# Half-size products on pairs of 512-column blocks and 8 of 16 chunks, one ring of weight buffers, and the running sum in DRAM

## The chip, the cores and the metric

The kernel runs on one core of one Trainium2 chip. The metric is the device time of one execution in microseconds (us); the median of three runs of the kernel before is 1694.32 us (1693.03 to 1695.05). A core has TensorE (PE, with its weight load PEld), VectorE (DVE), ScalarE (ACT), GpSimd (POOL) and SyncE (SP); each works through a queue of its own in order, and they wait for each other by semaphores. The big loads are issued by SP.

## The reference

One layer of a decoder trunk on 256 tokens of width D = 2048, in float32:

```python
proj = rmsnorm(x, attn_norm) @ w_in          # q, k, v of three mixers, and the gates (3 x 2048)
y_gla, y_sb, y_mem = (mixer(...) @ w_br for each of the three branches)
g = sigmoid(gates)
merged = g[0] * y_gla + g[1] * y_sb + g[2] * y_mem
x = x + merged @ w_o
gate, up = split(rmsnorm(x, ffn_norm) @ w_gate_up)      # 2 x 5632 columns
x = x + (silu(gate) * up) @ w_down
```

Nearly all the work is in products of 256 tokens with weight matrices that are read once from DRAM.

## The kernel before, in words

**Tiling.** Weights lie in blocks of 512 columns (NB); a chunk is 128 rows of a weight matrix. A block of `w_gate`, `w_o` or `w_gate_up` has 16 chunks, and `w_down` is taken in parts of 16, 16 and 12 chunks. Tokens are two halves of 128. The activation, stored transposed, is PE's stationary operand, the weights stream through.

**Precision.** Every float32 operand is split into a rounded part `h` (float32r) and a remainder `l`, and a product is three matmuls: h*h, h*l, l*h. For the weights this happens on the chip: `split` (L118) lets ScalarE cast a loaded tile to `wh` (L121) and VectorE subtract, `wl = raw - wh` (L122).

**Plain products.** `gemm` (L152) takes four chunks to a load (`raw`, 1 MB), two to a split of 1024 elements per partition, and issues 12 matmuls of 512 columns for each split.

**Products with fewer multiplications.** `sgemm` (L183) works on one block of 512 columns. Its first 6 chunks and the 256 tokens are cut in half every way (128 tokens, 3 chunks, 256 columns), and seven products of such halves stand for eight (the Winograd form of Strassen's method). The four quarters of the weights (`b11` to `b22`, tag `rq`, five buffers of 384 KB) are loaded apart, and VectorE adds them in place four times (L252, 768 elements per partition) between the splits. Each product (`prod`, L218) is 9 matmuls of 256 columns; the results are kept in `cv` by ScalarE and joined on VectorE at the block's end (L297, L302). The other 10 chunks of the block are done by `rest` (L230), as in a plain product. The sums on the token side, the forms, are made once for each activation by `make_forms` (L305) in two `raw` buffers.

**Order.** The program is written out in order; each engine's order comes from a scheduler of the framework that weighs the written order against its own times. `background` holds small jobs (transposes of finished pieces, the forms), and each product and each split of a gemm lets one step of them through (`step`, L98).

**Buffers.** `raw` has three slots. The pairs `wh`/`wl` have 4 buffers in the first stage (pool `wring`) and 6 in the later ones (pools `mrg` and `ffn`, released and made anew at L843, L896 and L900). PSUM holds 4 `acc` and 4 `tmp`.

**The stages the change touches.** The gates of two branches (L854 to L868): `sgemm` on a gate block, then a `gemm` with the branch's weights. The output product (L877 to L889), with the residual added into `x2`, which stays in SBUF. The FFN (L905 to L934): three parts, each with 4, 4 or 3 pairs of gate and up blocks, then that part of `w_down` added into `x2`; the last part (12 chunks) uses `gemm`.

Of the kernel before, what the change touches and what calls it, by code (L numbers as in the profile page):

```python
# [16 lines left out]
P = 128  # L17
# [13 lines left out]
SP = 3  # L31
HB = NB // 2
# [43 lines left out]
def trunk(ctx: ExitStack, tc: tile.TileContext, a, out):  # L76
# [5 lines left out]
    wp = ctx.enter_context(tc.tile_pool(name="wp", bufs=3))  # L82
    IT = 2 * NB
    small = ctx.enter_context(tc.tile_pool(name="small", bufs=2))
# [60 lines left out]
    def loads():  # L145
        return wp.tile([P, KG, NB], F32, tag="raw", name="raw", bufs=3)

    def parts():

        return [kit.tile([P, IT], F32R, tag=f"w{x}", name=f"w{x}", bufs=ring_bufs) for x in "hl"]  # L150

    def gemm(xs, w, c0, row0=0, first=(), load=nc.sync.dma_start):  # L152
# [9 lines left out]
        for n in sizes:  # L162
            xp = [x() if callable(x) else x for x in xs[k0 : k0 + n]]
            raw = loads()
            r0 = row0 + k0
            load(raw[:, :n], w[c0 // NB, :, r0 : r0 + n])
            for g in range(0, n, 2):
                m = min(2, n - g)
                wh, wl = (x[:].rearrange("p (k n) -> p k n", k=2) for x in parts())
                split(wh[:, :m], wl[:, :m], raw[:, g : g + m])  # L170
                for t in range(2):
                    s = slice(t * P, (t + 1) * P)
                    for j in range(m):
                        xh, xl = xp[g + j]
                        k = k0 + g + j
                        pe.matmul(o[t][:], xh[:, s], wh[:, j], start=k == 0, stop=False)  # L176
                        pe.matmul(o[t][:], xh[:, s], wl[:, j], start=False, stop=False)  # L177
                        pe.matmul(o[t][:], xl[:, s], wh[:, j], start=False, stop=k == nk - 1)  # L178
                step()
# [3 lines left out]
    def sgemm(xs, forms, w, blk, row0=0, late=False):  # L183
# [11 lines left out]
        o = [acc() for _ in range(2)]  # L195
        x = tmp()
        cv = kit.tile([P, 5, HB], F32, tag="cv", name="cv", bufs=2)
        wb = w[blk, :, row0 * NB : (row0 + nk) * NB]
        ob = 4 * SP * HB

        def quarter(i):
            q = kit.tile([P, SP * HB], F32, tag="rq", name="rq", bufs=5)
            nc.sync.dma_start(q[:], wb[:, i * SP * HB : (i + 1) * SP * HB])
            return q

        def form(src):
            hi, lo = (x[:, : SP * HB] for x in parts())
            split(hi, lo, src[:])
            return hi, lo

        def single(half, tok):
            s = slice(tok * P, (tok + 1) * P)
            return [[part[:, s] for part in xs[half * SP + i]] for i in range(SP)]

        def formed(f):
            return [[part[:, f, i] for part in forms] for i in range(SP)]

        def prod(dst, left, right, start=False, stop=False):  # L218
            hi, lo = right
            for i in range(SP):  # L220
                xh, xl = left[i]
                c = slice(i * HB, (i + 1) * HB)
                pe.matmul(dst, xh, hi[:, c], start=start and i == 0, stop=False, skip_group_check=True)  # L223
                pe.matmul(dst, xh, lo[:, c], start=False, stop=False, skip_group_check=True)  # L224
                pe.matmul(dst, xl, hi[:, c], start=False, stop=stop and i == SP - 1, skip_group_check=True)  # L225
            step()

        loaded = {}

        def rest(k0, last=False):  # L230

            if k0 not in loaded:
                n = min(KG, nk - k0)
                raw = loads()
                c = ob + (k0 - 2 * SP) * NB
                nc.sync.dma_start(raw[:, :n], wb[:, c : c + n * NB].rearrange("p (k n) -> p k n", n=NB))
                for g in range(0, n, 2):
                    loaded[k0 + g] = raw[:, g : g + 2]
            wh, wl = (x[:].rearrange("p (k n) -> p k n", k=2) for x in parts())
            split(wh, wl, loaded[k0])  # L240
            for t in range(2):
                s = slice(t * P, (t + 1) * P)
                for j in range(2):
                    xh, xl = xs[k0 + j]
                    f, e = k0 + j == 2 * SP, last and j == 1
                    pe.matmul(o[t][:], xh[:, s], wh[:, j], start=f, stop=False, skip_group_check=True)  # L246
                    pe.matmul(o[t][:], xh[:, s], wl[:, j], start=False, stop=False, skip_group_check=True)  # L247
                    pe.matmul(o[t][:], xl[:, s], wh[:, j], start=False, stop=e, skip_group_check=True)  # L248
            step()

        def add(dst, a, b):
            dve.tensor_tensor(dst[:], a[:], b[:], op=ALU.add)  # L252

        ks = list(range(2 * SP, nk, 2))
        x0, x1 = x[:, :HB], x[:, HB:]

        def some():
            if ks and not late:
                rest(ks[0], len(ks) == 1)
                ks.pop(0)  # L260

        if late:
            for j in ks:
                rest(j)
        some()
        b21 = quarter(0)
        prod(x0, single(1, 0), form(b21), start=True, stop=True)
        act.copy(cv[:, 2], x0)
        b11 = quarter(2)
        prod(o[0][:, :HB], single(0, 0), form(b11))  # L270
        b22 = quarter(1)
        some()
        add(b21, b21, b22)
        prod(x1, formed(1), form(b21), stop=True)
        b12 = quarter(3)
        prod(o[0][:, HB:], formed(0), form(b12), stop=late)
        some()
        add(b22, b22, b12)
        add(b12, b12, b21)
        prod(x0, formed(2), form(b12), stop=True)  # L280
        act.copy(cv[:, 4], x0)
        some()

        def p7():
            prod(x0, formed(3), form(b22), stop=True)
            act.copy(cv[:, 0], x0)

        def q4():
            add(b11, b11, b12)
            prod(o[1][:, :HB], single(0, 1), form(b11), stop=late)  # L290

        for f in (q4, p7) if late else (p7, q4):
            f()
        while ks and not late:
            some()

        dve.tensor_tensor(  # L297
            cv[:, 1:4:2], x1.unsqueeze(1).to_broadcast([P, 2, HB]), cv[:, 0:5:4], op=ALU.subtract
        )
        c = [cv[:, i : i + 2].rearrange("p a b -> p (a b)") for i in (2, 0)]  # L300
        for t in range(2):
            dve.tensor_tensor(c[t], o[t][:], c[t], op=ALU.add)  # L302
        return c

    def make_forms(parts, name):  # L305


        sf = [kit.tile([P, 4, SP, P], F32R, name=f"{name}{x}", bufs=1) for x in "hl"]

        def flat():  # L310
            return loads()[:].rearrange("p g n -> p (g n)")[:, : 2 * SP * T]

        def make():
            hw = flat().rearrange("p (k t) -> p k t", k=2 * SP)
            r = flat().rearrange("p (f i t) -> p f i t", f=4, i=SP)
            k = 0
            for h, l in parts:
                n = min(h.shape[1], 2 * SP - k)
                dve.tensor_tensor(hw[:, k : k + n], h[:, :n].bitcast(F32), l[:, :n].bitcast(F32), op=ALU.add)
                k += n  # L320
            yield
            a11, a12, a21, a22 = (hw[:, k * SP : (k + 1) * SP, i * P : (i + 1) * P] for i in range(2) for k in range(2))
            s3, s5, s6, s7 = (r[:, f] for f in range(4))
            dve.tensor_tensor(s5, a22, a21, op=ALU.subtract)
            dve.tensor_tensor(s7, a12, a22, op=ALU.subtract)
            dve.tensor_tensor(s6, s5, a12, op=ALU.subtract)
            dve.tensor_tensor(s3, a11, s6, op=ALU.add)
            yield
            split(sf[0][:], sf[1][:], r)
            yield  # L330

        background.append(make())
        return sf
# [27 lines left out]
    def token_rstd(name, src, r, n):  # L361

        ss = const.tile([P, 2], F32, name=f"{name}_ss")
        for t in range(2):
            x = loads()[:].rearrange("p g n -> p (g n)")
            nc.sync.dma_start(x, src[t * P : (t + 1) * P, :])
            act.activation(x, x, AF.Square, accum_out=ss[:, t : t + 1])
            yield
# [68 lines left out]
    kit = wring = tc.alloc_tile_pool(name="wring", bufs=1)  # L437
    ring_bufs = 4
# [33 lines left out]
    def load_consts():  # L472
        r = loads()[:].rearrange("p g n -> p (g n)")
        nc.sync.dma_start(r[:, :C_W], a["consts"])
        act.copy(cst[:], r[:, :C_R])
        act.copy(cr[:], r[:, C_R:C_W])
        yield
# [168 lines left out]
    raw = wp.tile([P, KD, P], F32, tag="raw", name="raw_a", bufs=3)  # L646
    nc.sync.dma_start(raw[:], a["w_ga"])
    p = tmp()
    for k0 in range(0, KD, 8):
        hi, lo = (x[:].rearrange("p (k n) -> p k n", k=8) for x in parts())  # L650
        split(hi, lo, raw[:, k0 : k0 + 8])
        for j in range(8):
# [190 lines left out]
    wring.release()  # L843

    kit = mrg = tc.alloc_tile_pool(name="mrg", bufs=1)
    ring_bufs = 6
    sx = make_forms([xtiles], "sx")
    background.append(gla_T())
    tm, later_on = [], []
    for b, w_br in ((1, "w_br_sb"), (0, "w_br_gla")):  # L850
# [3 lines left out]
        for n in range(0, D, NB):  # L854
            g = sgemm(xs, sx, a["w_gate"], (b * D + n) // NB, late=b == 1 and n == 0)
# [137 lines left out]
```

## Time and profile before

| | us |
|---|---|
| median of three runs | 1694.32 |
| profiled execution, its own time | 1692.7 |
| its span | 1690.9 |
| TensorE busy | 1673.7 |
| VectorE busy | 1286.2 |
| ScalarE busy | 930.7 |

The page's first part gives the busy time of each engine and its share of the span. In other views each row is a group of instructions (line, engine, operation, output and input tiles, shape, count, busy time, mean ns of one, and the idle time ahead of it with who ended it), or, in the timeline, one or a few instructions with their start and duration. A TensorE duration includes the pipeline and overlaps the next one's, and a VectorE operation can start a little before the one ahead of it ends; so steps are best read from start to start.

The first slice of the span (up to about 600 us) is plain gemms with the attention mixers beside them; then come the gates, the output product, and from about 960 us the FFN. The bytes moved are 322.05 MB at a mean of 190 GB/s.

### The profile page before, as it was taken

The page shows a single profiled execution, that of the slowest core. Times are in us where ns is not written, and L with a number is a line of the kernel's source. Part 1 is how long each engine was busy: PE and PEld are TensorE (multiplying, and loading weights), DVE is VectorE, ACT ScalarE, POOL GpSimd, SP SyncE. Part 2 cuts the span into 40 slices and gives each one's busy share as a digit, 9 for nine tenths or more (in the row PEclk, how much of TensorE's full clock was granted, in tenths as well). Part 3 has the DMA queues.
Part 4 walks back from the last instruction along what each step waited for, and adds up shares of the span by engine and source line. Part 5 has one row for each costly group of instructions (what it writes and reads, how often), then busy time and mean ns, then how long its engine had stood idle before and what let it go on. Part 6 is the DMA issues. An engine that isn't in the chain of part 4 may idle for free.

```text
span 1690.9 us, 22452 instructions
## 1 busy us (share of the span) xinstructions
PE 1673.7 (99%) x8730; PEld 1427.2 (84%) x8730; DVE 1286.2 (76%) x1585; ACT 930.7 (55%) x1231; POOL 1.3 (0%) x6
## 2 busy tenths in 40 slices
PE   8999999999999999999999999999999999999999
PEld 6888888888877888888888788888888888888887
DVE  6756566664665578877889899988889988888863
ACT  6654454664653455555556566665555565555642
POOL 0000000000000000000000000000000000000000
PEclk9999999999999999999999999999999999999999
DMA  8765445445534556564566364655564555565562
GB/s 326 265 235 188 149 152 191 156 151 198 173 129 146 199 211 213 185 233 165 184 213 202 123 225 137 236 199 199 199 200 162 196 193 186 198 206 192 178 224 100
DMA packets 68682, 322.05 MB, mean 190 GB/s; under 512 B 7504, under 2 KB 12112, under 8 KB 41440
## 3 DMA queue, kind: packets, MB, share of 16 engines
q1 hardware_dynamic: 68112, 320.17, 55.4%
q8 instruction: 68, 1.11, 0.3%
q10 hardware_dynamic: 464, 0.45, 0.1%
q14 instruction: 38, 0.31, 0.0%
HBM read 318.50 MB, written 2.10 MB: 190 GB/s over the span
## 4 chain that ended last, share of the span: by engine, by line
PE 96%; DVE 1%; DMA 1%; ACT 0%; issue 0%; SPq 0%; DVEq 0%; ACTq 0%
PE acc L176 13%; PE acc L177 13%; PE acc L178 13%; PE acc L247 11%; PE acc L248 11%; PE acc L246 11%; PE tmp L225 4%; PE tmp L224 3%; PE tmp L223 3%; PE acc L225 3%; PE acc L223 3%; PE acc L224 3%; PE tmp L336 2%; DVE wl L122 1%; DMA raw<-in_w_mem_kv 0%; PE tmp L565 0%
## 5 line engine op out<-in xcount | busy, mean ns | idle before, releaser
L122 DVE TENSOR_TENSOR wl<-raw,wh 128x1024 fp32r<-128x1024 f32 (+1 forms) x459 | 558.7, 1220 | 271.7 <-ACT wh L121 268.1
L121 ACT CAST wh<-raw 128x1024 fp32r<-128x1024 f32 (+1 forms) x459 | 480.0, 1048 | 426.6 <-PE acc L178 265.8
L121 ACT CAST wh<-rq 128x768 fp32r<-128x768 f32 x294 | 244.8, 837 | 206.5 <-PE acc L248 80.0
L122 DVE TENSOR_TENSOR wl<-rq,wh 128x768 fp32r<-128x768 f32 x294 | 278.9, 954 | 27.1 <-ACT wh L121 23.5
L176 PE MATMUL acc<-wh,xTh 128*128 128x512 f32 x576 | 230.3, 400 | 0.0
L178 PE MATMUL acc<-wh,xTl 128*128 128x512 f32 x576 | 225.0, 391 | 0.0
L177 PE MATMUL acc<-wl,xTh 128*128 128x512 f32 x576 | 224.6, 390 | 0.0
L246 PE MATMUL acc<-wh,hh 128*128 128x512 f32 x440 | 174.4, 398 | 4.2 <-ACT wh L121 4.2
L247 PE MATMUL acc<-wl,hh 128*128 128x512 f32 x440 | 174.5, 396 | 1.1 <-DVE wl L122 0.9
L248 PE MATMUL acc<-wh,hl 128*128 128x512 f32 x440 | 173.0, 393 | 0.0
L252 DVE TENSOR_TENSOR rq<-rq 128x768 f32<-128x768 f32 x168 | 160.7, 957 | 4.4
L176 PE MATMUL acc<-wh,oh 128*128 128x512 f32 x320 | 125.3, 393 | 2.9 <-ACT wh L121 2.0
L178 PEld LDWEIGHTS acc<-wh,xTl 128*128 128x128 f32 x576 | 108.1, 188 | 23.3 <-issue 0.3
L176 PEld LDWEIGHTS acc<-wh,xTh 128*128 128x128 f32 x576 | 108.3, 188 | 22.1 <-issue 1.4
L177 PEld LDWEIGHTS acc<-wl,xTh 128*128 128x128 f32 x576 | 108.4, 188 | 21.7 <-issue 0.7
L177 PE MATMUL acc<-wl,oh 128*128 128x512 f32 x320 | 125.5, 392 | 0.5 <-DVE wl L122 0.5
L178 PE MATMUL acc<-wh,ol 128*128 128x512 f32 x320 | 125.3, 392 | 0.0
L246 PEld LDWEIGHTS acc<-wh,hh 128*128 128x128 f32 x440 | 83.5, 190 | 20.0 <-ACT wh L121 4.9
L248 PEld LDWEIGHTS acc<-wh,hl 128*128 128x128 f32 x440 | 83.8, 190 | 18.1
L247 PEld LDWEIGHTS acc<-wl,hh 128*128 128x128 f32 x440 | 84.0, 191 | 16.6 <-DVE wl L122 2.2
L176 PEld LDWEIGHTS acc<-wh,oh 128*128 128x128 f32 x320 | 60.1, 188 | 17.8 <-ACT wh L121 2.5
L177 PEld LDWEIGHTS acc<-wl,oh 128*128 128x128 f32 x320 | 60.5, 189 | 13.8 <-DVE wl L122 1.1
(319 smaller groups left out, 2999.3 us busy)
## 6 DMA issues: line engine op xcount, KB each, us to landing
raw<-in_w_in SPq DMA_DIRECT2D x72, 1024.0 KB, 4.8
raw<-in_w_gate_up SPq DMA_DIRECT2D x44, 1024.0 KB, 4.9
rq<-in_w_gate_up SPq DMA_DIRECT2D x88, 384.0 KB, 4.9
raw<-in_w_down SPq DMA_DIRECT2D x28, 1024.0 KB, 4.8
raw<-in_w_gate SPq DMA_DIRECT2D x16, 1024.0 KB, 6.9
raw<-in_w_mem_kv SPq DMA_DIRECT2D x15, 1024.0 KB, 4.9
rq<-in_w_gate SPq DMA_DIRECT2D x32, 384.0 KB, 5.2
rq<-in_w_down SPq DMA_DIRECT2D x32, 384.0 KB, 4.7
```

The lines of the kernel that those rows point to most:

```text
L121: act.copy(hi, src)
L122: dve.tensor_tensor(lo, src, hi.bitcast(F32), op=ALU.subtract)
L176: pe.matmul(o[t][:], xh[:, s], wh[:, j], start=k == 0, stop=False)
L177: pe.matmul(o[t][:], xh[:, s], wl[:, j], start=False, stop=False)
L178: pe.matmul(o[t][:], xl[:, s], wh[:, j], start=False, stop=k == nk - 1)
L223: pe.matmul(dst, xh, hi[:, c], start=start and i == 0, stop=False, skip_group_check=True)
L224: pe.matmul(dst, xh, lo[:, c], start=False, stop=False, skip_group_check=True)
L225: pe.matmul(dst, xl, hi[:, c], start=False, stop=stop and i == SP - 1, skip_group_check=True)
L246: pe.matmul(o[t][:], xh[:, s], wh[:, j], start=f, stop=False, skip_group_check=True)
L247: pe.matmul(o[t][:], xh[:, s], wl[:, j], start=False, stop=False, skip_group_check=True)
L248: pe.matmul(o[t][:], xl[:, s], wh[:, j], start=False, stop=e, skip_group_check=True)
L252: dve.tensor_tensor(dst[:], a[:], b[:], op=ALU.add)
```

## The change

`sgemm` now takes two blocks at once, and cuts 8 chunks, 256 tokens and 1024 columns in half: 128 tokens, 4 chunks, 512 columns, so that a half of the columns is one block. `SP` is 4 in place of 3. The last part of `w_down` goes through `sgemm` too. The quarters are now ordinary `raw` loads of 1 MB; the weights in DRAM need no other layout for it.

```diff
-    def sgemm(xs, forms, w, blk, row0=0, late=False):
+    def sgemm(xs, forms, w, blks, row0=0, late=False, plus=None):
...
+        o = {(t, j): acc() for t in range(2) for j in range(2)}
+        x0, x1 = tmp(), tmp()
...
+        def prod(dst, left, b, last, *sums, gone=()):
+
+
+            for g in (0, 2):
+                for to, of in sums:
+                    x, y = (q[i][0][:, g : g + 2] for i in (to, of))
+                    dve.tensor_tensor(x, x, y, op=ALU.add)
+                wh, wl = half(q[b][0], g)
+                for i in range(2):
+                    mm(dst, left[g + i], wh[:, i], wl[:, i], last and (g, i) == (2, 1))
...
+        if late:
+            seq = [(p1,), (p2,), *r0[:2], *r1[:2], (p5,), (p3,), *r0[2:3], (p6,), *r0[3:], (p7,), (q4,), *r1[2:]]
+        else:
+            seq = [x for n, p in enumerate((p1, p5, p3, p6)) for x in ((p,), *r0[n : n + 1])]
+            seq += [(p2,), (p7,), *r1[:1], (q4,), *r1[1:]]
```

A product is now 12 matmuls of 512 columns in two halves of 6, with one split of 1024 elements (two chunks) for each half; a sum is two additions of 1024 elements. `rest` is called per block and two chunks. The forms are made in four pieces of 512 elements and split one by one.

The buffers: `raw` and `wh`/`wl` come from rings that live to the end and are widened where a stage has room: 3 slots and 4 pairs at the start, 2 slots and 1 pair more for the gates and the output product, 1 pair more for the FFN. A slot goes back to a list when its last split is written down in the program.

```diff
+    widen("ring1", 3, 4)
...
-        return wp.tile([P, KG, NB], F32, tag="raw", name="raw", bufs=3)
+
+        slot = free_raw.pop(0)
+        buf = slot[0].tile([P, KG, NB], F32, tag="raw", name="raw", bufs=slot[1])
+        return buf, lambda: free_raw.append(slot)
...
+    widen("ring2", 2, 1)
...
+    widen("ring3", 0, 1)
```

The running sum x2 goes to DRAM (`x2d`) from GpSimd's queue; the first two parts of `w_down` are added to it there by the transfer, and the last part reads it back.

```diff
+                nc.gpsimd.dma_start(x2d[:, t, n : n + NB], v)
...
+            x2s = [kit.tile([P, D], F32, tag=f"sf{x}", name="x2s", bufs=1) for x in "hl"]
+            for t in range(2):
+                nc.gpsimd.dma_start(x2s[t][:], x2d[:, t])
...
-                for t in range(2):
-                    v = x2[:, t, n : n + NB]
-                    dve.tensor_tensor(v, v, o[t], op=ALU.add)
-                continue
-            o = gemm(fs, wd, n, row0=4 * part[0])
...
+                    if not final:
+                        nc.gpsimd.dma_start(x2d[:, t, n : n + NB], result(t), accum_op=ALU.add)
```

In `w_o` and in the last part of `w_down`, what is added to the product (`plus`: the residual, or `x2s`) is added to the kept pieces ahead of the end (L297 of the new kernel).

Three places in the engines' order. The first is VectorE in the FFN, in the first part, where one block follows another; before, from the last sums (L252) of a gate block to the first sums of the up block after it:

```order
L252 TENSOR_TENSOR rq_8435<-rq_8435,rq_8358 128x768
L252 TENSOR_TENSOR rq_8381<-rq_8381,rq_8435 128x768
L122 TENSOR_TENSOR wl_8471<-rq_8435,wh_8470 128x768
L122 TENSOR_TENSOR wl_8485<-raw_8450,wh_8484 128x1024
L122 TENSOR_TENSOR wl_8501<-rq_8403,wh_8500 128x768
L122 TENSOR_TENSOR wl_8516<-rq_8381,wh_8515 128x768
L122 TENSOR_TENSOR wl_8531<-raw_8528,wh_8530 128x1024
L122 TENSOR_TENSOR wl_8558<-raw_8555,wh_8557 128x1024
L122 TENSOR_TENSOR wl_8576<-rq_8573,wh_8575 128x768
L252 TENSOR_TENSOR rq_8573<-rq_8573,rq_8604 128x768
```

The same place in the new kernel, from the last splits of a pair of blocks (`raw_7957` is its fourth quarter, `raw_8004` and `raw_8064` its last rest halves) to the first sums (L246) of the next pair (`raw_8111` and `raw_8167` its first quarters, `raw_8142` its first rest halves):

```order
L132 TENSOR_TENSOR wl_8035<-raw_7957,wh_8034 128x1024
L132 TENSOR_TENSOR wl_8067<-raw_8064,wh_8066 128x1024
L132 TENSOR_TENSOR wl_8083<-raw_8064,wh_8082 128x1024
L333 TENSOR_TENSOR cv_7999<-acc_7775,cv_7999 128x512
L132 TENSOR_TENSOR wl_8114<-raw_8111,wh_8113 128x1024
L132 TENSOR_TENSOR wl_8124<-raw_8111,wh_8123 128x1024
L132 TENSOR_TENSOR wl_8145<-raw_8142,wh_8144 128x1024
L246 TENSOR_TENSOR raw_8111<-raw_8111,raw_8167 128x1024 x2
L333 TENSOR_TENSOR cv_7939<-acc_7774,cv_7939 128x512
L132 TENSOR_TENSOR wl_8171<-raw_8111,wh_8170 128x1024
```

What moved: three splits of the next pair now stand ahead of the add (L333, `cv_7939`) that needs the end of the old pair on PE; sums and splits are all 1024 wide, and the 768-wide ones are gone.

The second place is SP, which issues the loads of the same pair; `raw_8142` takes the slot of `raw_7957`:

```order
L224 DMA raw_8064<-in_w_gate_up 128x2048
L224 DMA raw_8111<-in_w_gate_up 128x2048
L224 DMA raw_8167<-in_w_gate_up 128x2048
L224 DMA raw_8142<-in_w_gate_up 128x2048
L224 DMA raw_8219<-in_w_gate_up 128x2048
```

The scheduler has put the second quarter of the new pair (`raw_8167`) ahead of its first rest halves.

The third place is VectorE where the forms (`sd`) of the first part of `w_down` are made; before, in one block of operations (L319 to L327 and the split into `sdl`):

```order
L319 TENSOR_TENSOR raw_8841<-fh_8752,fl_8753 128x512
L122 TENSOR_TENSOR fl_8753<-tmp_8816,fh_8752 128x512
L324 TENSOR_TENSOR raw_8842<-raw_8841 128x384
L325 TENSOR_TENSOR raw_8842<-raw_8841 128x384
L326 TENSOR_TENSOR raw_8842<-raw_8842,raw_8841 128x384
L327 TENSOR_TENSOR raw_8842<-raw_8841,raw_8842 128x384
L122 TENSOR_TENSOR sdl_8755<-raw_8842,sdh_8754 128x1536
L122 TENSOR_TENSOR wl_8883<-raw_8880,wh_8882 128x1024
```

And in the new kernel (L343 makes the four forms in `cv` pieces; `wl_8270` is the split of a product that PE is due to run):

```order
L343 TENSOR_TENSOR cv_8182<-cv_8197,cv_8182 128x512
L246 TENSOR_TENSOR raw_8167<-raw_8167,raw_8219 128x1024
L343 TENSOR_TENSOR cv_8197<-cv_8195,cv_8197 128x512
L132 TENSOR_TENSOR sd_8104<-cv_8182,sd_8104 128x512
L343 TENSOR_TENSOR cv_8195<-cv_8182,cv_8195 128x512
L132 TENSOR_TENSOR sd_8104<-cv_8197,sd_8104 128x512
L343 TENSOR_TENSOR cv_8180<-cv_8180,cv_8195 128x512
L132 TENSOR_TENSOR sd_8104<-cv_8195,sd_8104 128x512
L246 TENSOR_TENSOR raw_8219<-raw_8219,raw_8111 128x1024
L132 TENSOR_TENSOR sd_8104<-cv_8180,sd_8104 128x512
L246 TENSOR_TENSOR raw_8167<-raw_8167,raw_8219 128x1024
L132 TENSOR_TENSOR wl_8270<-raw_8219,wh_8269 128x1024
```

The forms now stand between the sums of a running product and ahead of its split.

More of the change, by code (lines that the diff above doesn't have):

```diff
@@ L81, in trunk, with widen @@
     const = ctx.enter_context(tc.tile_pool(name="const", bufs=1))
-    wp = ctx.enter_context(tc.tile_pool(name="wp", bufs=3))
     IT = 2 * NB
+    dram = ctx.enter_context(tc.tile_pool(name="dram", bufs=1, space=bass.MemoryType.DRAM))
+    free_raw, splits, turn = [], [], [0]
+    def widen(name, raw, w):
+        pool = ctx.enter_context(tc.tile_pool(name=name, bufs=1, side="right", reuse_waits="tile"))
+        free_raw.extend([(pool, raw)] * raw)
+        splits.extend([(pool, w)] * w)
+    widen("ring1", 3, 4)
     small = ctx.enter_context(tc.tile_pool(name="small", bufs=2))
@@ L163, in gemm @@
             xp = [x() if callable(x) else x for x in xs[k0 : k0 + n]]
-            raw = loads()
+            raw, done = loads()
             r0 = row0 + k0
@@ L181, in gemm @@
         return o
-    def sgemm(xs, forms, w, blk, row0=0, late=False):
+    def sgemm(xs, forms, w, blks, row0=0, late=False, plus=None):
         nk = len(xs)
[L195 to L213, printed above, removed]
-        def formed(f):
[L216 to L225, printed above, removed]
-            step()
[L228 to L240, printed above, removed]
-            for t in range(2):
[L242 to L260, printed above, removed]
-        if late:
[L263 to L303, printed above, removed]
@@ new lines, in sgemm, with load, mm @@
+        x0, x1 = tmp(), tmp()
+        c, q, loaded, begun = {}, {}, {}, set()
+        def load(j, k):
+            raw, done = loads()
+            n = min(KG, nk - k)
+            nc.sync.dma_start(raw[:, :n], w[blks[j], :, row0 + k : row0 + k + n])
+            return raw, done
+        def mm(dst, xp, wh, wl, last):
+            xh, xl = xp
+            pe.matmul(dst[:], xh, wh, start=id(dst) not in begun, stop=False, skip_group_check=True)
+            begun.add(id(dst))
+            pe.matmul(dst[:], xh, wl, start=False, stop=False, skip_group_check=True)
+            pe.matmul(dst[:], xl, wh, start=False, stop=last, skip_group_check=True)
@@ new lines, in half @@
+        def half(raw, g):
+            wh, wl = (x[:].rearrange("p (k n) -> p k n", k=2) for x in parts())
+            split(wh, wl, raw[:, g : g + 2])
+            return wh, wl
+        def prod(dst, left, b, last, *sums, gone=()):
[6 more added lines that the diff above has]
+                    mm(dst, left[g + i], wh[:, i], wl[:, i], last and (g, i) == (2, 1))
+                if g:
+                    for i in gone:
+                        q[i][1]()
+                step()
@@ new lines, in single, with keep, p1, p2 @@
+        def single(h, t):
+            return [[x[:, t * P : (t + 1) * P] for x in xs[h * SP + i]] for i in range(SP)]
+        def formed(f):
+            return [[x[:, f, i] for x in forms] for i in range(SP)]
+        def keep(at):
+            c[at] = piece()
+            act.copy(c[at][:], x0[:])
+        def p1():
+            q[21] = load(0, SP)
+            prod(x0, single(1, 0), 21, False)
+            keep((0, 0))
+        def p2(last):
+            q[11] = load(0, 0)
+            prod(o[0, 0], single(0, 0), 11, last)
@@ new lines, in p3, with q4, p5, p6 @@
+        def p3(last):
+            q[12] = load(1, 0)
+            prod(o[0, 1], formed(0), 12, last)
+        def q4(last):
+            prod(o[1, 0], single(0, 1), 11, last, (11, 12), gone=(11, 12))
+        def p5():
+            q[22] = load(1, SP)
+            prod(x1, formed(1), 21, True, (21, 22))
+        def p6():
+            prod(x0, formed(2), 12, False, (22, 12), (12, 21), gone=(21,))
+            keep((0, 1))
+        def p7():
+            prod(x0, formed(3), 22, True, gone=(22,))
+            keep((1, 0))
+            c[1, 1] = piece()
+            dve.tensor_tensor(c[1, 1][:], x1[:], c[1, 0][:], op=ALU.subtract)
+            dve.tensor_tensor(c[0, 1][:], x1[:], c[0, 1][:], op=ALU.subtract)
+            for at, p in (plus or {}).items():
+                dve.tensor_tensor(c[at][:], c[at][:], p, op=ALU.add)
@@ new lines, in rest @@
+        def rest(j, k, last):
+            if (j, k) not in loaded:
+                raw, done = load(j, k)
+                loaded.update({(j, k + g): (raw, g, done if g or k + 2 == nk else None) for g in (0, 2)})
+            raw, g, done = loaded[j, k]
+            wh, wl = half(raw, g)
+            if done:
+                done()
+            for t in range(2):
+                for i in range(2):
+                    xp = [x[:, t * P : (t + 1) * P] for x in xs[k + i]]
+                    mm(o[t, j], xp, wh[:, i], wl[:, i], (t, j) in last and i == 1)
+            step()
@@ new lines, in sgemm, with result @@
+        done = []
+        for n, (f, *args) in enumerate(seq):
+            left = {at for later in todo[n + 1 :] for at in later}
+            last = [at for at in todo[n] if at not in left]
+            f(*args, *([last] if args else [bool(last)] if f in into else []))
+            for j in range(2):
+                if j not in done and (1, 1) in c and not {(0, j), (1, j)} & left:
+                    done.append(j)
+                    def result(t, dst=None, cols=slice(0, NB), j=j):
+                        d = c[t, j][:] if dst is None else dst
+                        dve.tensor_tensor(d[:, cols], o[t, j][:, cols], c[t, j][:, cols], op=ALU.add)
+                        return d[:, cols]
+                    yield j, result
```

219 lines of the change are left out of this document (125 added, 94 removed).

## The prediction

> **What bounds the kernel now.** I read the page's totals first, then the chain of work that ended last, then the busy times in stretches of 100 us.
>
> ```profile
> span 1690.9 us, 22452 instructions
> PE 1673.7 (99%) x8730; PEld 1427.2 (84%) x8730; DVE 1286.2 (76%) x1585; ACT 930.7 (55%) x1231; POOL 1.3 (0%) x6
> PE 96%; DVE 1%; DMA 1%; ACT 0%; issue 0%; SPq 0%; DVEq 0%; ACTq 0%
> ```
>
> TensorE is busy for 99% of the span and the chain runs on it for 96%. But 76% for VectorE is a mean over unlike stages, and the edit works in the later ones.
>
> ```profile
> 200.00:300.00 100.00, 100.00 (x464) 82.99 (x463) 62.46 (x91) 47.56 (x59) 0.00 (x0) 1.00 0.50 170
> 1200.00:1300.00 100.00, 100.00 (x581) 88.51 (x580) 89.65 (x100) 58.61 (x77) 0.00 (x0) 1.00 0.58 192
> 1400.00:1500.00 100.00, 100.00 (x585) 88.69 (x584) 90.54 (x103) 55.84 (x72) 0.00 (x0) 1.00 0.55 186
> PE acc L246 <- ACT wh L121: 5.9, 4, 2.0
> PE acc L247 <- DVE wl L122: 1.4, 2, 0.9
> ```
>
> The columns are stretch, length, then busy time of PE, PEld, DVE, ACT, POOL, the granted clock (full speed), the DMA share and GB/s. In the FFN (1200 to 1500) PE has no gap, yet VectorE is at 90%, where it was at 62% in the plain gemms. PE's waits for a weight part in `sgemm` come to 5.9 + 1.4 = 7.3 us in all. So PE sets the end, with VectorE one tenth behind: what the edit saves on PE counts only where VectorE can still follow.
>
> **PE's side.** The page's durations overlap (a 512-wide matmul lasts 0.39), so I take the step from start to start.
>
> ```profile
> 1207.04 0.39 PE L248 MATMUL acc<-wh,fl 128*128 128x512 f32 x1
> ...
> 1209.99 0.28 PE L223 MATMUL tmp<-wh,fh 128*128 128x256 f32 x1
> ...
> 1211.90 0.28 PE L224 MATMUL acc<-wl,fh 128*128 128x256 f32 x1
> 1056.93 0.60 PE L336 MATMUL tmp<-cst,cv 128*128 128x128 f32 x4
> 1057.29 0.36 PE L223 MATMUL acc<-wh,hh 128*128 128x256 f32 x1
> 1057.49 0.28 PE L224 MATMUL acc<-wl,hh 128*128 128x256 f32 x1
> ```
>
> Between 1207.04 and 1209.99 lie 13 steps of 512 columns: 0.2269 us each. Between 1209.99 and 1211.90 lie 16 steps of 256: 0.1194, more than half of 0.2269, so narrow products pay a surcharge. Four transposes take 0.36, and the matmul after them 0.08 more than its 0.12: 0.44.
>
> A pair of blocks with 16 chunks was 120 wide matmuls and 126 narrow: 27.2 + 15.0 = 42.3. It becomes 84 + 96 = 180 wide: 40.8, which saves 1.43. There are 21 such pairs (4 gates, 2 of `w_o`, 11 gate-up, 4 of `w_down`): 30.0. The last part of `w_down` (12 chunks) was a plain gemm of 288 wide matmuls and becomes 2 x 132: 24 x 0.2269 = 5.4. **PE's work falls by 35.5 us.**
>
> **VectorE's side.**
>
> ```profile
> 1074.85 0.69 DVE L297 TENSOR_TENSOR cv<-tmp,cv 128x512 f32<-128x512 f32 x1
> 1075.46 0.95 DVE L122 TENSOR_TENSOR wl<-rq,wh 128x768 fp32r<-128x768 f32 x1
> 1076.32 1.22 DVE L122 TENSOR_TENSOR wl<-raw,wh 128x1024 fp32r<-128x1024 f32 x1
> 1077.46 1.50 DVE L302 TENSOR_TENSOR cv<-acc,cv 128x512 f32<-128x512 f32 x2
> 1078.88 1.82 DVE L122 TENSOR_TENSOR wl<-rq,wh 128x768 fp32r<-128x768 f32 x2
> 1080.62 1.94 DVE L252 TENSOR_TENSOR rq<-rq 128x768 f32<-128x768 f32 x2
> 1082.47 1.22 DVE L122 TENSOR_TENSOR wl<-raw,wh 128x1024 fp32r<-128x1024 f32 x1
> 1083.61 0.95 DVE L122 TENSOR_TENSOR wl<-rq,wh 128x768 fp32r<-128x768 f32 x1
> 1054.37 1.41 DVE L913 SCALAR_TENSOR_TENSOR cv<-cv,r 128x512 f32<-128x512 f32 x2
> 1055.69 0.95 DVE L122 TENSOR_TENSOR wl<-rq,wh 128x768 fp32r<-128x768 f32 x1
> ```
>
> Again from start to start: a split of 1024 takes 1.14, of 768 0.87, a sum of 768 0.925 (two take 1.85), an operation of 512 0.61, the scaled product 0.66. A sum of 1024 isn't in the trace: between a split of its size (1.14) and 4/3 of the smaller sum (1.23); I take 1.20, the smaller sum plus the step between the two splits, 0.27.
>
> A gate-up pair before: 10 splits of 1024, 14 of 768, 8 sums, eight operations of 512 and two scaled products: 11.4 + 12.2 + 7.4 + 4.9 + 1.3 = 37.2. PE needs 42.3 plus eight transposes (0.88): 43.15. That is 86%, near the 90% of the windows. After: 22 splits, 8 sums, the same ten small ones: 25.1 + 9.6 + 6.2 = 40.9 against 41.7 on PE. **Of six us of slack, 0.8 are left.** For the others: a `w_down` pair 38.3 against 40.8, so that VectorE gains ground; a `w_o` pair, with four more sums (L297) and eight transposed pieces, 38.3 + 2.4 + 3.2 = 44.0 against 40.8 + 16 transposes = 42.6; a pair of the last part, 18 splits, 8 sums and ten of 512, 36.2 against 29.95, where the plain gemm had 24 splits in 65 us. The gates' pairs stand beside two gemms each and have room. The pieces (`hl`) are counted by this row, less the 0.08 that overlaps:
>
> ```profile
> L125 DVE SCALAR_TENSOR_TENSOR hl<-tmp,vecs,hh 128x256 fp32r<-128x256 f32 x16 | 7.4, 478 | 0.0
> ```
>
> The forms (`make_forms`) become 12 operations of 512, 7.3 us of VectorE, six times: for the gates, for `w_o` (under a gemm), at the start of the FFN, and once in each part, the last one new.
>
> **A wait that is added.** The first load of rest halves in a pair (`raw_8142` in the SP rows shown) takes the slot that the fourth sum's last split (`wl_8035`) frees, and its split `wl_8145` stands five VectorE operations later: 4 x 1.14 + 0.61 = 5.2 us.
>
> ```profile
> raw<-in_w_gate_up SPq DMA_DIRECT2D x44, 1024.0 KB, 4.9
> raw<-in_w_gate SPq DMA_DIRECT2D x16, 1024.0 KB, 6.9
> raw<-in_w_gate_up SPq DMA_DIRECT2D x22, 512.0 KB, 5.3
> L121 ACT CAST wh<-raw 128x1024 fp32r<-128x1024 f32 x457 | 478.7, 1050 | 425.3 <-PE acc L178 265.8 <-PE acc L248 122.0 <-PE acc L225 7.4
> ```
>
> The load lands after 4.9 to 6.9, the cast takes 1.05. Another load stands straight ahead of it in the queue, so I take 5.3, the row of loads issued close behind others: VectorE waits 5.3 + 1.05 - 5.2 = 1.2 us in every pair (0.8 at 4.9, 2.8 at 6.9). Behind `wl_8145` on VectorE stand two sums, the add that ends the old pair and the next product's splits, and PE waits for those. A gate-up pair then costs VectorE 42.06: 0.3 more than PE.
>
> **Where PE then waits.** First gate-up pair: 42.06 + 7.3 - 41.72 = 7.6. The three others with forms: 7.6 in the first part; in the second and third 5.6, since two `w_down` pairs ahead give a lead of 2 x 1.3, less two pairs at 0.3. The three left over: 0.3 each. Last part: 2 x (36.2 + 1.2) - 59.9 = 14.9, less 3.1 that follows the last split and 2.0 of work which PE has queued on entering and not on leaving: 9.8. Together 37.1. `w_o`: 2 x 2.6 = 5.1. The gates' first pair: 38.3 + 7.3 - 40.8 = 4.8. In all 47.0; the 7.3 of before go.
>
> **Parts that I cost at nothing.** The stores of x2 move to POOL's queue, sixteen of them adding in DRAM. No such transfer is in the trace; the nearest row is a plain store of 256 KB:
>
> ```profile
> out<-x SPq DMA_DIRECT2D x6, 256.0 KB, 2.6
> ```
>
> Between 2.6 and, by the 1 MB loads, 6.9 us, and the piece that it reads is needed a pair, some 41 us, later. The two loads of `x2s` (1 MB each) have from the last use of `sf` to the first `L297`, more than half a pair; if they came 5 us late, 5 would be lost once. The ring that outlives its stages takes away pool waits, which sit inside the 7.3. ScalarE's casts come to 22 x 1.05 = 23 us of a pair's 42.
>
> **Sum.** -35.5 + 47.0 - 7.3 = +4.2 on the profiled execution's own 1692.7 us (1690.9 of span and 1.8 around it): 1696.9. The median of the runs, 1694.32, is 1.6 above that execution, so I forecast **1698**. With the load at 4.9 the waits come to 40.1 and the time to 1692, with the sums at 1.14 besides to 31.5 and 1683; with the load at 5.9 to 58 and 1709.
>
> **Rivals.** (1) VectorE keeps up, and it gets faster. If the load is there in time (landing under 4.1) and the sums cost 1.14, a gate-up pair is 40.4, VectorE gains 1.3 in each and its lead, at most the three splits ahead of the first add that waits for PE (5.4 us of PE's work), covers nearly all of the later forms: waits 6.0 + 4.7 + 0.6 + 0.6, 6.4 at the end, 1.8 in `w_o`, 4.3 in the gates, 24.4 in all; -35.5 + 24.4 - 7.3 = -18.4, **1676**. For it: PE lost only 7.3 us to an engine at 90%. Against it: the counts above leave 2%. (2) The raw loads decide, and it gets slower. At 6.9 from issue to landing each pair waits 2.8: 1.9 over PE in seven plain gate-up pairs and four with forms (9.2 each), 1.2 in `w_down`, 13 at the end, 8.3 and 4.8 ahead: 77.4, so +34.6, **1729**. It decides from a landing of about 5.0 on. For it: five slots of 1 MB, four of them held by one product's quarters, in place of eight buffers; against it: the DMA share of 0.55 to 0.58. (3) VectorE doesn't overlap its operations, when each waits for a cast from another engine. Then a 1024 costs the mean duration in these rows, not 1.14:
>
> ```profile
> L122 DVE TENSOR_TENSOR wl<-raw,wh 128x1024 fp32r<-128x1024 f32 x457 | 557.4, 1223 | 271.7 <-ACT wh L121 268.1 <-PE tmp L729 1.3
> L302 DVE TENSOR_TENSOR cv<-acc,cv 128x512 f32<-128x512 f32 x84 | 57.3, 686 | 1.9 <-PE acc L248 1.4
> ```
>
> A gate-up pair is then 30 x 1.223 + 8 x 0.686 + 1.5 + 1.2 = 44.9, 3.2 over PE; the waits counted as before come to 107 and the time to **1759**. The rows at 1076.32 and 1082.47 speak against it: the next one starts 1.14 on. [...]
>
> **Chances.** Forecast (1683 to 1709) 0.52, of which 0.10 faster by over 0.2%, 0.20 within, 0.22 slower; 0.2%, about 3.4 us, is what a measurement of this kernel can tell from no change. Rival 1 (1668 to 1683) 0.22; rival 2 (1709 to 1735) 0.23; rival 3 0.03. That makes 0.32 faster, 0.20 the same, 0.48 slower. The range, 1677 to 1720, leaves out a tenth at each end: half of rival 1, and the far half of rival 2 with rival 3. The forecast's own range is 1683 to 1709.
>
> **What would show it.** PE's instructions fall to about 7300 and its wide step stays at 0.227; VectorE's busy share in the FFN rises from 90% to 96% or more; PE's waits for `wl` and `wh` grow from 7 to over 40 us, in the pairs with forms and in the last 75 us. Waits of ScalarE's cast for a gate-up load tell rival 2, VectorE with gaps in plain gate-up pairs rival 1, steps of 1.22 rival 3. I am wrong in the mechanism if PE waits under 25 us in all and the time falls all the same, or if PE's step changes.

## The result, and the profile after

| | before | after |
|---|---|---|
| median, us | 1693.76 (1693.03 to 1695.05) | 1715.03 (1714.35 to 1715.77) |
| profiled execution: its own time, span | 1692.7, 1690.9 | 1714.35, 1712.6 |

The changed kernel is slower: the ratio is 1.0125, with a 95% interval of 1.0107 to 1.0142. That lies inside the range, but 17 us above the forecast, and the terms of the sum show that it got there by another way: PE's work fell far less than forecast and its waits grew less, and that the two errors partly cancel is luck.

The page of the changed kernel: span, totals and chain, as they were shown of before.

```profile
span 1712.6 us, 19224 instructions
PE 1678.6 (98%) x7320; PEld 1344.5 (79%) x7320; DVE 1391.6 (81%) x1607; ACT 966.0 (56%) x1163; POOL 20.5 (1%) x32
PE 86%; DVE 10%; ACT 2%; issue 1%; DMA 0%; SPq 0%; DVEq 0%; ACTq 0%
```

PE has 1410 matmuls fewer, which was to save 35.5 us, and is busy for 4.9 us longer. VectorE's part of the chain went from 1% to 10%. The same three stretches of 100 us, and PE's waits for weight parts in `sgemm`, after the change:

```profile
200.00:300.00 100.00, 100.00 (x454) 81.71 (x454) 62.41 (x92) 46.38 (x58) 0.00 (x0) 1.00 0.48 163
1200.00:1300.00 100.00, 100.00 (x436) 81.13 (x435) 93.65 (x89) 59.28 (x62) 5.08 (x6) 1.00 0.64 197
1400.00:1500.00 100.00, 100.00 (x436) 81.16 (x435) 94.68 (x92) 60.80 (x65) 4.67 (x6) 1.00 0.69 227
```

```profile
PE tmp L230 <- ACT wh L131: 10.6, 9, 2.1
PE acc L230 <- ACT wh L131: 6.2, 10, 1.6
PE acc L232 <- DVE wl L132: 4.6, 7, 1.5
PE tmp L232 <- DVE wl L132: 4.3, 6, 1.1
```

The waits are 25.7 us where 47.0 were predicted and 7.3 stood before. The line that explains the loss is the first: from 200 to 300 us both kernels run the same plain gemms, both show PE busy for all of the 100 us at a clock of 1.00, and one got through 464 matmuls, the other through 454. "Busy 100%" hides it; only the count tells. The timeline of the changed kernel in the FFN has the step:

```profile
1199.90 0.40 PE L233 MATMUL acc<-wh,fl 128*128 128x512 f32 x1
...
1203.38 0.39 PE L233 MATMUL acc<-wh,fl 128*128 128x512 f32 x1
```

Between these two rows lie 15 steps: 3.48 / 15 = 0.232. Over all wide matmuls on weight parts that another wide one follows without a stall (a step under 0.26 us) the mean step is 0.2279 before and 0.2325 after, and after the change it is the same in every stretch of the run (0.2324 to 0.2327 in stretches of 200 us). Traffic of the DMA engines is not the cause, as a late window of the changed kernel shows, where they moved nothing at all (share 0.00, the column ahead of the last):

```profile
1690.00:1700.00 10.00, 9.93 (x43) 7.73 (x41) 9.67 (x12) 4.29 (x6) 0.00 (x0) 1.00 0.00 0
```

43 matmuls in 9.93 us are 0.231 each. Nor is it the other engines: the 150 or so steps during which both VectorE and ScalarE rested have a mean of 0.2324 after, and 0.2272 before.

PE's whole time can be laid out by such steps: **work** is the sum of undisturbed steps (a disturbed one counts with its usual length), **lost** is all above that. The span itself grew by 21.7; the rest lies ahead of the first matmul and behind the last.

| change against before, us | predicted | after |
|---|---|---|
| PE's work | -35.5 | -4.5 |
| lost: waits, stalls, half clock | +39.7 | +25.5 |
| sum | +4.2 | +21.0 |

### The profile page after: what moved, and what is told of

It is laid out like the page before. It is cut to its first block, busy times and chain, and to the rows that moved or that the text cites. A ratio compares the mean times of both kernels' runs of the same rounds, so it can differ in the third digit from the quotient of the medians.

```text
span 1712.6 us, 19224 instructions
## 1 busy us (share of the span) xinstructions
PE 1678.6 (98%) x7320; PEld 1344.5 (79%) x7320; DVE 1391.6 (81%) x1607; ACT 966.0 (56%) x1163; POOL 20.5 (1%) x32
## 4 chain that ended last, share of the span: by engine, by line
PE 86%; DVE 10%; ACT 2%; issue 1%; DMA 0%; SPq 0%; DVEq 0%; ACTq 0%
PE acc L196 12%; PE acc L197 12%; PE acc L198 12%; PE acc L232 11%; PE acc L230 11%; PE acc L233 11%; PE tmp L232 4%; PE tmp L233 4%; DVE wl L132 4%; PE tmp L230 4%; DVE raw L246 3%; ACT wh L131 1%; PE tmp L377 1%; DVE cv L343 1%; PE tmp L580 0%
## 5 line engine op out<-in xcount | busy, mean ns | idle before, releaser
L131 ACT CAST wh<-raw 128x1024 fp32r<-128x1024 f32 (+1 forms) x725 | 750.7, 1049 | 641.0 <-PE acc L198 294.4
L132 DVE TENSOR_TENSOR wl<-raw,wh 128x1024 fp32r<-128x1024 f32 (+1 forms) x725 | 866.5, 1218 | 238.6 <-ACT wh L131 236.2
L246 DVE TENSOR_TENSOR raw<-raw 128x1024 f32<-128x1024 f32 x184 | 219.7, 1218 | 1.0
L232 PE MATMUL acc<-wl,fh 128*128 128x512 f32 x208 | 82.3, 397 | 2.3 <-DVE wl L132 2.3
L230 PE MATMUL acc<-wh,fh 128*128 128x512 f32 x208 | 81.8, 397 | 1.5 <-ACT wh L131 1.5
L233 PE MATMUL acc<-wh,fl 128*128 128x512 f32 x208 | 81.8, 395 | 0.0
```

Source lines behind the costliest of these rows:

```text
L131: act.copy(hi, src)
L132: dve.tensor_tensor(lo, src, hi.bitcast(F32), op=ALU.subtract)
L230: pe.matmul(dst[:], xh, wh, start=id(dst) not in begun, stop=False, skip_group_check=True)
L232: pe.matmul(dst[:], xh, wl, start=False, stop=False, skip_group_check=True)
L233: pe.matmul(dst[:], xl, wh, start=False, stop=last, skip_group_check=True)
L246: dve.tensor_tensor(x, x, y, op=ALU.add)
```

## Experiments: where does PE's longer step come from?

**Theory.** The one thing that I found different in the first stage is the place of its tiles in SBUF, the core's on-chip memory. Per partition, in the compiled programs, `wh` and `wl` (the moving operand) began at 608 modulo 1024 before and begin at 992 after, when their ring moved to the other end; `raw` began at a multiple of 64 and now does not; all stationary operands (`xTh`, `xTl`, forms, pieces) lie at 96 modulo 512 in both. Rival: the order of instructions or their semaphores. Six kernels move things by empty bytes and change nothing else. The first three have this edit, with n = 384, 32 and 224:

```diff
+    pad = ctx.enter_context(tc.tile_pool(name="pad", bufs=1, side="right"))
+    pad.tile([P, n // 4], F32, name="pad")
     widen("ring1", 3, 4)
```

> The changed kernel with 384 bytes per partition left empty ahead of its ring, so that the weight parts lie at 608 modulo 1024 as before the change and not at 992; nothing else moves. Theory L (the place of the ring in SBUF lengthens PE's wide step, 0.227 to 0.232): the step comes back to 0.227 to 0.229, PE's work falls by some 6700 x 0.0045 = 30 us, VectorE then has as little slack as I predicted and PE's waits for weight parts grow from 26 to about 45 us: 1698 us (1690 to 1706). If VectorE isn't that near: 1683. Rival N (the step comes from the order of instructions or from their semaphores, not from addresses): step 0.232, 1715.

> The changed kernel with 32 bytes left empty ahead of the ring: raw buffers and parts begin at multiples of 64 bytes (960 modulo 1024). Theory L-64 (what costs is that the raw buffers no longer begin at a multiple of 64, as they did before the change): step 0.227, time as in the run with 384 bytes, about 1698. Theory L-1024 (what counts is the place of the parts against that of the stationary operand, modulo 1 KB): 960 is near 992, step about 0.232, 1715. Rival N: 1715.

> The changed kernel with 224 bytes left empty: parts at 768 modulo 1024, a multiple of 256, raw buffers at a multiple of 64. L-64: 0.227, about 1698. L-1024: a place between, step between 0.227 and 0.232, 1698 to 1715. Rival N: 1715.

The fourth puts the bytes into the kernel before, ahead of `wring`, `mrg` and `ffn`:

```diff
+    pad1 = tc.alloc_tile_pool(name="pad1", bufs=1)
+    pad1.tile([P, 96], F32, name="pad")
     kit = wring = tc.alloc_tile_pool(name="wring", bufs=1)
```

> The kernel before with 384 bytes left empty ahead of the pools that hold its weight parts in each stage, so that they lie at 992 modulo 1024 as after the change; raw buffers stay where they were. Theory L-1024: PE's wide step goes from 0.228 to 0.232 with no change in the work: 5496 x 0.0045 = 25 us and some for the narrow steps, 1719 (1712 to 1728). L-64 (raw buffers) and rival N: 1694.

After these four, two more asked whether the address or the distance counts, and what its period is: the 384 bytes ahead of `const`, at the left end, and 128 bytes at the right end.

> The changed kernel with the 384 empty bytes at the other end, ahead of the constants: the weight parts (moving operand) stay at 480 modulo 512, where the step was 0.2325, and all stationary operands (x transposed, forms, pieces) move from 96 to 480 modulo 512. Theory D (only the distance between the two operands counts: fast at 0 modulo 512): step 0.227 to 0.228, time 1686 (1682 to 1690). Theory A (the parts' own address counts): step 0.232, 1715.

> The changed kernel with 128 bytes left empty ahead of its ring: parts at 352 modulo 512, distance to the stationary operands 256 modulo 512. Distances so far: 0 gave 0.2273, 384 gave 0.2325, 352 gave 0.2334, 160 gave 0.2342. If the period is 256: step 0.227, 1686. If it is 512: step 0.233 to 0.235, 1715 to 1727.

The distance below is that of the moving from the stationary operand modulo 256; the step is the mean of all undisturbed neighbours, as above.

| kernel | parts, mod 512 | stationary, mod 512 | distance, mod 256 | step, us | median, us | ratio to before (95%) |
|---|---|---|---|---|---|---|
| before | 96 | 96 | 0 | 0.2279 | 1693.76 | 1 |
| after | 480 | 96 | 128 | 0.2325 | 1715.03 | 1.0107 to 1.0142 |
| after + 384 (e1) | 96 | 96 | 0 | 0.2273 | 1685.68 | 0.9938 to 0.9963 |
| after + 32 (e2) | 448 | 96 | 96 | 0.2334 | 1720.05 | 1.0139 to 1.0167 |
| after + 224 (e3) | 256 | 96 | 160 | 0.2342 | 1725.80 | 1.0172 to 1.0202 |
| before + 384 (e4) | 480 | 96, some 480 | 128, some 0 | 0.2320 | 1712.39 | 1.0091 to 1.0118 |
| after, left + 384 (e5) | 480 | 480 | 0 | 0.2273 | 1683.93 | 0.9929 to 0.9954 |
| after + 128 (e6) | 352 | 96 | 0 | 0.2273 | 1687.22 | 0.9942 to 0.9967 |

The windows of 200 to 300 us, of the fourth, the first, the fifth and the sixth kernel in this order, show it in a count:

```profile
200.00:300.00 100.00, 100.00 (x454) 81.47 (x453) 61.88 (x93) 46.50 (x60) 0.00 (x0) 1.00 0.47 159
```

```profile
200.00:300.00 100.00, 100.00 (x462) 82.99 (x461) 63.07 (x91) 48.33 (x60) 0.00 (x0) 1.00 0.50 173
```

```profile
200.00:300.00 100.00, 100.00 (x464) 82.98 (x463) 62.52 (x90) 48.30 (x60) 0.00 (x0) 1.00 0.51 171
```

```profile
200.00:300.00 100.00, 100.00 (x464) 82.99 (x463) 62.42 (x92) 47.42 (x58) 0.00 (x0) 1.00 0.50 169
```

Not all came as expected. e1 got its step back, but its time fell to 1685.7 and not to 1698 (1690 to 1706): VectorE was not that near. e2 and e3 kept the long step, which theory L-64 had coming back, and in e3 it is longer still, where L-1024 had it shorter; e4 has the step and the lower edge of the time (1712) that L-1024 gave. Theory D, that only the distance of the two operands counts, was made from these four; e5 then tested it, and e6 its period, and it held in both (1683.9 and 1687.2, where 1686 was expected). The parts' own address does not decide (480 is slow in the changed kernel and fast in e5), nor does the alignment of `raw` to 64 bytes (e2 and e3 have it and are the slowest). So theory L-64 falls, and of L-1024 the distance stays but not its period: 256 is as fast as 0, so the period is 256, as far as the distances tried tell. Within the fourth kernel the same rule splits the steps: 0.2326 where the stationary operand stayed at 96, and 0.2282 for the 729 steps whose stationary tile had moved along to 480. The fourth kernel also shows that the price has nothing to do with the rest of the change: the kernel before, with its work and order untouched, loses 1.05%.

So the change without this accident makes the kernel **faster**, by about 0.5% (e1, e5, e6). The difference of after and e1 is 29.4 us.

## Experiments: the rest of the sum, with the operands at distance 0

In e1 the step is as I had assumed, so the other terms can be read. PE's waits, and ScalarE's for a gate-up load, in e1:

```profile
PE tmp L232 <- ACT wh L133: 11.2, 9, 2.2
PE acc L232 <- ACT wh L133: 6.3, 10, 1.6
PE tmp L234 <- DVE wl L134: 5.6, 6, 1.3
PE acc L234 <- DVE wl L134: 5.1, 8, 1.5
...
ACT wh L133 <- DMA raw<-in_w_gate_up: 8.3, 3, 5.0
```

The waits are 28.2 in all, against 47.0. ScalarE's cast waited for a gate-up load three times in the whole run, not once in every pair. VectorE's timeline in a gate-up pair of e1:

```profile
1110.07 4.63 DVE L248 TENSOR_TENSOR raw<-raw 128x1024 f32<-128x1024 f32 x4
1114.62 9.17 DVE L134 TENSOR_TENSOR wl<-raw,wh 128x1024 fp32r<-128x1024 f32 x8
1123.70 2.35 DVE L248 TENSOR_TENSOR raw<-raw 128x1024 f32<-128x1024 f32 x2
```

Four sums of 1024 take 4.55 us from start to start, 1.14 each, as long as a split (9.08 / 8 = 1.135). A gate-up pair is then 30 x 1.135 + 4.9 + 1.3 = 40.25 on VectorE, and a test is to take its room away:

```diff
                 wh, wl = half(q[b][0], g)
+                if b in (11, 12) and g == 0 and w is a["w_gate_up"] and not sums:
+                    dve.tensor_tensor(wl, q[b][0][:, :2], wh.bitcast(F32), op=ALU.subtract)
```

> The changed kernel with 384 empty bytes (1685.7), and in each of the eleven gate-up pairs two more VectorE operations of 1024 columns: the subtraction that makes wl is done twice for the first half of two products. 2 x 1.135 x 11 = 25.0 us of VectorE. By my prediction's count (VectorE 0.3 slower than PE in each pair) all of it is paid: 1711. By the durations of the run with 384 bytes (sums of 1024 at 1.135, a pair 40.25 on VectorE plus its wait for the raw load, against 41.7 on PE) about 1 us of a pair is free and 11 x 1.2 = 13 us are paid: 1699 (1693 to 1704). If VectorE has room that I don't see (2.3 or more per pair): 1686.

Measured 1698.90, with a ratio of 1.0023 (1.0013 to 1.0033) to before; its nine runs lie between 1694.9 and 1700.9. Of the 25.0 us added, 13.2 were paid, so 11.8 were free, 1.07 a pair in the mean. That is the second expectation, 1699, and VectorE is ahead of PE and not 0.3 a pair behind it. But 1.07 is not the room of each pair. Taken from one matmul to the 180th wide one after it, a gate-up pair that nothing holds up takes 40.8 to 41.8 us in e1, no more than PE's own 41.7. In e7's profiled execution the two pairs right behind each two `w_down` pairs are no longer than in e1, so the work added there was free; the second pair of the FFN is 2.7 us longer, and the last part of `w_down`, where nothing was added, 4.6.

**The last part of `w_down`.** It goes back to plain gemms, and the sum that is read back from DRAM is added to their results:

```diff
-            if len(tiles) == 2:
+            if len(tiles) == 2 and part[-1] < NF - 1:
...
+        for n in range(0, D if final else 0, NB):
+            o = gemm(fs, a["w_down"], n, 4 * part[0])
...
-        for n0 in range(0, D, 2 * NB):
+        for n0 in range(0, 0 if final else D, 2 * NB):
```

> The changed kernel with 384 empty bytes, and the last part of w_down by plain gemms again (288 wide matmuls more per four blocks than 2 x 132 have; no forms for it). PE's work rises by 24 x 0.2273 = 5.5. By my prediction's waits (5.6 for the forms of that part, 9.8 at the end) 15.4 go: 1676. By the waits measured in the run with 384 bytes (3.4 and 6.7, and the half clock after the first, 3.4) 13.5 go: 1678. If the waits at the end are not VectorE's but the tail's own, only forms and clock go, 6.8: 1684.

Measured 1675.97, ratio 0.9894 (0.9881 to 0.9908): the fastest kernel of this study that leaves nothing out, 1.1% under the kernel before. Taking this part of the change back gains 9.7 us, though PE does 5.5 more. It doesn't tell the two first expectations apart (1676 and 1678), but the third, 1684, falls.

**The sum in DRAM.** The sixteen adding transfers are left out:

```diff
-                        nc.gpsimd.dma_start(x2d[:, t, n : n + NB], result(t), accum_op=ALU.add)
+                        result(t)
```

> The changed kernel with 384 empty bytes (1685.7), without the sixteen transfers that add the first two parts of w_down in DRAM: the output lacks these parts. The VectorE additions that feed them stay. My prediction cost these transfers at nothing: 1685.7 within 0.2%. If they delay the raw loads or hold VectorE's pieces, the time falls, by at most what PE still waits in the pairs around them (the form pairs at 1068 and 1325, about 4 us each): 1678 or more.

Measured 1688.72, ratio 0.9971 (0.9959 to 0.9982), 3.0 us over e1 (0.18%): no gain from taking them away, so they cost nothing that this measurement tells. In the profiled executions each pair of the FFN up to the last part takes the same time with and without them, to 0.1 us; the last part, behind all of them, is 3.4 us longer in e9, and there its clock was at half for 3.4 us, which e1's was not (mean granted clock of the run 0.991, of e1 0.992). Why stays open.

**The forms and the half clock.** Only the first forms of `w_down` are made:

```diff
-            if len(tiles) == 2:
+            if len(tiles) == 2 and part[0] == 0:
```

> The changed kernel with 384 empty bytes (1685.7), with the forms of the first part of w_down used in all three: the second and third are not made (24 VectorE operations of 512 fewer, and the products of these parts are wrong). In the trace PE waited about 3.4 us in each of the two gate-up pairs with forms, and the clock was at half for 6.8 us right behind each, another 3.4. If the half clock follows from PE's gaps, both go: 1685.7 - 2 x 6.8 = 1672. If it comes by itself, only the waits go: 1679. If the waits are not the forms': 1685.7.

Measured 1670.37, ratio 0.9864 (0.9849 to 0.9879): 15.3 us less, 7.7 for each set of forms. In the profiled executions the two pairs take 48.8 and 48.9 us with forms and 41.8 without, as long as a pair that never had any. So waits and half clock both go, as the first expectation had it, and the half clock goes with the gaps. The windows around a pair with forms in e1 (first fence, with a full stretch as its last row), and that stretch in e10:

```profile
1064.00:1068.00 4.00, 4.00 (x19) 3.12 (x17) 4.00 (x7) 1.73 (x3) 0.00 (x0) 1.00 0.00 0
1068.00:1072.00 4.00, 0.67 (x2) 0.19 (x1) 4.00 (x5) 2.19 (x3) 0.00 (x0) 1.00 0.00 0
1072.00:1076.00 4.00, 3.22 (x8) 1.76 (x9) 4.00 (x5) 2.74 (x3) 0.00 (x0) 0.64 0.44 121
1076.00:1080.00 4.00, 4.00 (x11) 3.13 (x10) 2.97 (x3) 2.45 (x4) 0.00 (x0) 0.51 0.90 307
1080.00:1084.00 4.00, 4.00 (x19) 3.26 (x19) 3.74 (x4) 1.31 (x3) 0.00 (x0) 1.00 0.60 190
...
1300.00:1400.00 100.00, 96.64 (x419) 78.54 (x418) 97.36 (x103) 59.96 (x68) 0.00 (x0) 0.97 0.49 179
```

```profile
1300.00:1400.00 100.00, 99.61 (x451) 81.88 (x450) 96.78 (x97) 60.67 (x67) 0.00 (x0) 1.00 0.50 179
```

From 1068 to 1072 PE works for 0.67 of 4 us while VectorE works without a break; in the next two rows the granted clock is 0.64 and 0.51, and from 1076 to 1080 PE is "busy" all the time and gets through 11 matmuls where 19 are usual. In e10 the stretch from 1300 has neither the gap nor the dip. PE's waits ahead of the dip, in e1:

```profile
1070.35 0.50 PE L232 MATMUL tmp<-wh,sfh 128*128 128x512 f32 x1 [2.18 <-ACT wh L133]
1072.15 0.50 PE L234 MATMUL tmp<-wl,sfh 128*128 128x512 f32 x1 [1.29 <-DVE wl L134]
```

So ahead of this dip stand two waits of 2.2 and 1.3 us with one matmul between them, which leave PE idle for 3.3 us in the row from 1068. Not every gap is followed by a dip: in the changed kernel PE is busy for 17.27 us from 640 to 660, and the clock is 1.00 there and in the 20 us behind it.

The 3.4 us that I put on each half clock (6.8 us at 0.5) are an upper bound, for a PE that works all through it: 10 to 12 steps fell into each of these stretches, about 2 us more than at full clock, and the gaps cost the other 5 or so of the 7. Nor is the length of the dip fixed: by the granted clock in rows of 5 us, the dip of the changed kernel from 1090 to 1100 (0.58 and 0.74) comes to 6.8 us at half, the one from 1350 to 1360 (0.86 and 0.80) to 3.4.

## Why the prediction came out as it did

**The step that failed.** "PE's work falls by 35.5 us", with "its wide step stays at 0.227". I had named a change of PE's step as what would make the mechanism wrong, and that is what happened: 0.2325, because the ring's move had put the weight parts 128 bytes (modulo 256) from the stationary operands. Between e1 and the changed kernel, which differ in nothing else, PE's work rises by 34.5 us (-39.0 against -4.5) and the time by 29.4, since a slower PE waits less for VectorE (lost time +25.5, in e1 +32.6). I read the diff of the pools for waits and sizes and gave the ring's move to the other end of SBUF no price; the place of the tiles could have been compared ahead of the run, but no row of before told that it mattered.

**Term by term, where the step is 0.227 (e1).** PE's work falls by 39.0 (predicted 35.5). The 3.5 more are the step of before: I took 0.2269 from one clean stretch, the mean was 0.2279, and e1 has 0.2273; 5500 x 0.0006 = 3.3. Lost time rises by 32.6 (predicted 39.7), and the sum is -6.4 against +4.2.

**VectorE's side.** A second step failed here: the wait of 1.2 us for the raw load "in every pair". It rests on `raw_8142` taking the slot of `raw_7957`, free after `wl_8035`, and that reading was wrong. In the compiled program `raw_8142` has the address of `raw_8004`, whose last split, `wl_8049`, stands ahead of `wl_8035`. The trace of the changed kernel shows the same:

```profile
1053.38 2.35 DVE L132 TENSOR_TENSOR wl<-raw,wh 128x1024 fp32r<-128x1024 f32 x2
1054.62 0.33 SPq L224 DMA_DIRECT2D raw<-in_w_gate_up  x1
1056.85 3.48 DVE L132 TENSOR_TENSOR wl<-raw,wh 128x1024 fp32r<-128x1024 f32 x3
1061.00 3.48 DVE L132 TENSOR_TENSOR wl<-raw,wh 128x1024 fp32r<-128x1024 f32 x3
```

The first row begins with `wl_8049`, which ends at 1054.59; the load of `raw_8142` is issued at 1054.62, long before `wl_8035`, the first of the third row, ends at 1058.06. Its own split `wl_8145`, the last of the fourth row, starts at 1063.27. That is 8.7 us behind the slot's release, and although this load landed late (ScalarE waited 1.6 us for it), VectorE's splits follow each other without a gap. From the end of `wl_8035` it would have been 5.2. Without this wait VectorE's pair is 40.9 by my own figures, 0.8 under PE's. The other size that was off is the sum of 1024: 1.135 and not 1.20, the lower bound that I gave. The loads landed in 5.0, 4.9 and 4.9 (rows below), of my 4.9 to 6.9. My own variant, with the load at 4.9 and the sums at 1.14, said waits of 31.5 and 1683 us; e1 has 28.2 and 1685.7, near it, but by luck as far as the load goes, since it was not the landing that took the wait away. DMA issues and the sums' row after the change:

```profile
raw<-in_w_gate_up SPq DMA_DIRECT2D x88, 1024.0 KB, 5.0
raw<-in_w_down SPq DMA_DIRECT2D x44, 1024.0 KB, 4.9
raw<-in_w_gate SPq DMA_DIRECT2D x32, 1024.0 KB, 4.9
x2d<-cv POOLq DMA_DIRECT2D x16, 256.0 KB, 4.8
x2s<-x2d POOLq DMA_DIRECT2D x2, 1024.0 KB, 11.5
L246 DVE TENSOR_TENSOR raw<-raw 128x1024 f32<-128x1024 f32 x184 | 219.7, 1218 | 1.0
```

**Where PE waits.** The places were right: the gates' first pair, `w_o` (1.8 where I had 5.1), the first FFN pair, the pairs with forms, and the last part. Each real wait of a pair with forms was about half (3.4 to 4.5 where I had 5.6 to 7.6), but a cost that I had left out stands behind it, the half clock. Together 7.0 in the trace, by e10's median 7.7: right in sum, for an incomplete reason. Over the run the mean clock is 0.996 before and 0.992 in e1, so at most 0.004 x 1685 = 7 us of the lost time is the clock's; the listed waits make 20.9 (28.2 less 7.3), which leaves some 5 us or more that I can't assign.

**The last part.** 5.4 saved, 9.8 at the end and 5.6 for its forms: by my terms the edit loses 10.0. Taking it back gained 9.7.

**Costed at nothing.** The sixteen adding transfers: shown by e9. The loads of `x2s` took 11.5 us in the median, longer than the raw loads, and no wait on them stands in the trace. That the ring itself, apart from its place, costs nothing was not tried by itself.

**The rivals.** (1) VectorE keeps up, 1676: half right, for the change at distance 0 alone, whose 1685.7 lies between this rival and my forecast; the sums cost 1.14, as it asked, but the landing is 4.9 to 5.0 and not under 4.1. (2) The raw loads decide: the time, 1715, falls into this rival's range by luck. It is out, by the waits of ScalarE's cast for a gate-up load, four of 8.3 us in all after the change and three in e1, where it needed one in every pair. (3) VectorE doesn't overlap: out, since the operations last 1.22 (L246) and start 1.135 apart. And the rival that was missing, a longer matmul, decided.

## What to carry to other kernels

Where an edit moves pools, compare the addresses of the matmuls' two operands before and after: with weights and activations that keep one distance modulo 256 bytes, a few empty bytes in one pool set it for the whole run (128 bytes in e6: 1687.22 us in place of 1715.03), and the price of a distance of 128 in place of 0 (29.4 us between the changed kernel and e1) was larger here than what the edit won without it (about 8 us in e1). Compare the step of an untouched stage first, by matmuls per 100 us, since "busy" does not show it (464 and 454, both with PE busy for 100.00). And read the granted clock behind an engine's short gaps: a burst of VectorE work in one pair of e1 cost 7.0 us where the profile lists waits of 3.4 to 4.5, and the clock behind those of the first such pair was at 0.64 and 0.51. Last, where a sum hangs on which slot a load takes, read the slot from the compiled program's addresses.

## What the runs showed of the hardware

The step of a float32r matmul of 512 columns was 0.227 to 0.228 us where the moving and the stationary operand lay 0 modulo 256 bytes apart in a partition (before, e1, e5, e6, and part of e4), and 0.2325 at 128 (after), 0.2334 at 96 (e2) and 0.2342 at 160 (e3); other distances were not tried, and no run shows what in the hardware makes it. Over these eight layouts PE's own step went with the distance of its two operands, with VectorE and ScalarE at rest too (0.2272 before, 0.2324 after).
